# A decoder kernel on one core: first chunk in rounds, an output projection part, index queries and top-k rounds moved

## The chip, the cores and the metric

The kernel runs on one core of a Trainium2 chip, as one program. The metric is the device time of one execution in microseconds (us), lower is better. Five engines work from queues of their own and meet through semaphores: PE (TensorE matmuls; its weight loads are listed apart as PEld), DVE (VectorE), ACT (ScalarE), POOL (GpSimd) and SP (SyncE, which issues most DMAs). Each engine executes its own queue in order.

## What is computed

Two decoder layers over 512 tokens of width 1024 in float32, each a token mixer, a cross-attention into 256 memory tokens and a SwiGLU FFN, with a layer norm behind each. The mixer of layer 0 is latent attention (16 heads, low-rank queries and keys with RMS norms); that of layer 1 is sparse attention, where an indexer chooses 128 keys for each query:

```python
def mla_mixer(x, pos, w_in, q_norm, w_uq, kv_norm, w_ukv, w_o):
    h = x @ w_in                                  # c_q 512, c_kv 256, k_rope 32
    q = (rms_norm(c_q, q_norm) @ w_uq).reshape(b, s, 16, 64 + 32)
    kv = (rms_norm(c_kv, kv_norm) @ w_ukv).reshape(b, s, 16, 64 + 64)
    ...
    out = dense_causal_attention(q, k, v, (64 + 32) ** -0.5)
    return out.reshape(b, s, 16 * 64) @ w_o

def dsa_mixer(x, pos, rel_bias, w_in, w_o):
    h = x @ w_in                                  # q, k, v, 8 index queries, index key, weights
    ...
        dots = einsum('bqhd,bkd->bqhk', qi_blk, k_idx) * (64 ** -0.5)
        score = einsum('bqh,bqhk->bqk', wi_blk, relu(dots))
        score = where(causal, score, -inf)
        _, sel = lax.top_k(score, 128)
        ...
        logits = where(sel_ok, q_blk . k_sel * 64 ** -0.5 + rel_bias[bucket], -inf)
        o = softmax(logits) . v_sel
    return out @ w_o
```

## The kernel before

Every float32 product is made of three passes of a reduced type. `split` (ACT rounds to the high part, L104; a subtraction gives the low part, L106, on DVE or POOL) prepares an operand, and `mm3` (L137, L138, L139) adds high x high, high x low (or low x high) and the third. A weight chunk takes this path from DRAM: `raw` (a DMA), `wh` (ACT), `wl` (DVE or POOL). `bank("a")` and `bank("b")` are PSUM tiles (named `ps`), `t2` and `t8` SBUF tiles, `sm` small columns.

The code is handed to a scheduler at compile time, which sets the order of each engine's queue from a cost model and the data's dependences; `behind(ins)` pins an instruction after another in that order. The stages that the change touches, with their times in the profile:

- Start (0 to 20 us). `WARM` identity products on PE while the first DMAs land, then the first chunk: 4 token tiles times 8 chunks k of the width, 128x304 products into four banks (`ps2`).
- Latent norms (20 to 60 us). `rms_t` squares on ACT, takes the root on POOL, scales on DVE (L615) and transposes on PE (L618); `mla_v(i)` are value products. `rms_scaled`, the last scaled tile (`scaled[0]`), pins the split of a weight chunk that comes next (`wl_126`).
- Output projection of layer 0 (about 180 to 240 us). `out_proj_parts` is a generator that yields once, behind the products of its first weight chunk (c == 0); its caller continues it after the last heads' value products (L762, L763).
- Indexer (about 770 to 800 us). For each of four pairs j of index heads: a query projection (24 products), a split of the queries (`stack_q`), and scores for the query tiles qt = 1, 2, 3 (L1130, L1131); ACT takes the Relu (L1133), DVE adds them up into the tile's score (L1137).
- Top-k and sparse attention (about 800 to 935 us). The 128 largest of a row are taken away in 16 rounds of eight for each of qt = 1, 2, 3 (widths 256, 384, 512): `nc.vector.max` (L1149, MAX8 in the profile) and `match_replace` (L1150), on DVE, each reading what the one before left. `todo` holds the 48 rounds in order; 4 go before the key projections, `NTK[j]` before each query projection j = 0 to 7, the rest (`NTI` = 2 at a time) in the loop over n. `make_mask(qt)` (ACT, L1156) turns a finished tile into a mask.

Attention works on 16 items s0 to s15, item 4 qt + g for query tile qt and key head g, each of four query heads. Four names carry an item: `s` (scores: for each of the four heads a mask product L1205 where qt > 0, then L1206 and L1207 into a bank of ring "b", which has four; DVE reduces each bank, L498: scale, bias, row minimum; ACT takes the exponential, L505), `t` (transposes L1220 on PE into ring "a", split by L104 and L106), `p` (value products L1251, L1252; then L1254 on ACT, L1259 and L1263 on DVE). The score bank of one item comes free when DVE has reduced it, and the next item's products go there. `dsa_bias` loads the item's bias by a DMA from SP (L1186) into a `t8` tile. `steps` and `seq` order the items: s0 ... t2 s4, p2 t4 s5 behind the last query projections (j = 7), then s3, s6, s7, s8 and so on.

Of the kernel before, what the change touches and what calls it, by code (L numbers as in the profile page):

```python
# [15 lines left out]
ALU = mybir.AluOpType  # L16
# [7 lines left out]
NT = S // P  # L24
# [11 lines left out]
BIG = 2.0 ** 100  # L36
TOPK = 128
GW = 640
WARM = 8
NV = 256 + 8 + 64  # L40
NC0 = 256 + 32 + 16

# [27 lines left out]
def tile_hybrid_mla_dsa_deepnorm_block(ctx: ExitStack, tc: tile.TileContext, A: dict, out: bass.AP):  # L70
# [26 lines left out]
    def behind(ins):  # L97
        return tc.issue_after(ins.ins) if ins else ExitStack()

    high, low, load, power, scaled = ([None] for _ in range(5))  # L100

    def split(h, l, src, eng=None, after=None, copy_after=None):
        with behind(copy_after):
# [199 lines left out]
    def k_of(tiles, k):  # L303
        h, l = tiles[k // 4]
        return h[:, k % 4], l[:, k % 4]
# [87 lines left out]
    def out_proj_parts(src, w, kc, first, pins=(), pool=0):  # L393

        nk = 2 * kc

        def weights(n, c):
            pin = pins[kc * n + c] if pins else (None, None)
            return chunk(w(n, c), (P, 2, 512), nc.gpsimd if pin[1] or kc * n + c < pool else None, pin)

        for n in range(2):
            ws = [weights(n, c) for c in range(kc)] if n else None
            if n == 0:
                ps = [bank("b") for _ in range(NT)]
                for c in range(kc):
                    wh, wl = weights(n, c)
                    for i in range(2):
                        k = 2 * c + i
                        sh, sl = src(k)
                        for tt in range(NT):  # L410
                            ts_ = slice(P * tt, P * tt + P)
                            mm3(ps[tt], (sh[:, ts_], sl[:, ts_]), (wh[:, i], wl[:, i]), k == 0, k == nk - 1)
                    if c == 0:
                        norm = yield
                for tt in range(NT):
                    residual(ps[tt], tt, n, first)
                    if norm:
                        norm.stat(tt, n)
            else:
                for tt in range(NT):  # L420
                    ts_ = slice(P * tt, P * tt + P)
                    parts = TAIL if norm.last and tt == NT - 1 else ((0, 512),)
                    for c0, c1 in parts:
                        p1 = bank("b")
                        for k in range(nk):
                            sh, sl = src(k)
                            wh, wl = ws[k // 2]
                            mm3(p1[:, c0:c1], (sh[:, ts_], sl[:, ts_]), (wh[:, k % 2, c0:c1], wl[:, k % 2, c0:c1]), k == 0, k == nk - 1)
                        early = len(parts) > 1
                        if tt and c0 == 0 and not early:  # L430
                            norm.finish(tt - 1)
                        residual(p1, tt, n, first, c0, c1)
                        norm.stat(tt, n, c0, c1)
                        if c0 == 0 and early:
                            norm.finish(tt - 1)
                norm.finish(NT - 1)
# [53 lines left out]
    class Softmax:  # L490
# [4 lines left out]
        def exp(self, i, src, scale, in1=None, after=None):  # L495
            Sx, nb = self.parts[i], self.nb[:, i:i + 1]
            if in1 is not None:
                nc.vector.tensor_tensor_reduce(out=Sx, in0=src, in1=in1, op0=ALU.add, op1=ALU.min,  # L498
                                               scale=-scale, scalar=3e38, accum_out=nb)
                src, scale = Sx, -1.0  # L500
            else:
                nc.vector.tensor_reduce(nb, src, axis=AX.X, op=ALU.max)
                nc.vector.tensor_scalar(nb, nb, -scale, None, op0=ALU.mult)
            with behind(after):
                nc.scalar.activation(Sx, src, AF.Exp, bias=nb, scale=scale, accum_out=self.sm[:, i:i + 1])  # L505
# [15 lines left out]
    def ts_of(tt):  # L521
        return slice(P * tt, P * tt + P)
# [46 lines left out]
    for c in range(4):  # L569
        h, l = XT[c // 2]  # L570
        rx = raw_x[c // 2]
        step = 1 if c == 0 else 2
        for i in range(0, 2, step):
            k0 = 2 * (c % 2) + i
            split(h[:, k0:k0 + step], l[:, k0:k0 + step], rx[:, k0:k0 + step])
            if 2 * c + i in w_parts:
                t, a, b = w_parts[2 * c + i]
                split(whs[t][:, a:b], wls[t][:, a:b], raw_w[t][:, a:b])
        for i in range(2):
            k = 2 * c + i  # L580
            xh, xl = k_of(XT, k)
            for tt in range(NT):
                ts_ = ts_of(tt)
                mm3(ps2[tt][:, 0:NC0], (xh[:, ts_], xl[:, ts_]), (whs[k // 3][:, k % 3], wls[k // 3][:, k % 3]),
                    k == 0, k == NK - 1)
    steps = trig()
    next(steps)
    krs = []
# [55 lines left out]
    for tt in range(NT):  # L644
# [14 lines left out]
        if tt == 2:  # L659
            ka = t2()  # L660
            kb_ = t2()
            nc.vector.tensor_tensor(ka[0:64], pk[0:64], TK[0:64], op=ALU.mult)
            nc.vector.tensor_tensor(kb_[0:64], pk[64:128], TK[64:128], op=ALU.mult)
            nc.vector.tensor_tensor(ka[0:64], ka[0:64], kb_[0:64], op=ALU.add)
    for hv in range(5):
        mla_v(hv)
    rms_t(psq[NT - 1], 512, NT - 1, gq, cq)
    rms_end = high[0], low[0]
    rms_power, rms_scaled = power[0], scaled[0]

    K8 = [t8(), t8()]
    for i, k8 in enumerate(K8):
# [442 lines left out]
    KIA, KIB = t2(FR), t2(FR)  # L1115
    split(KIA, KIB, pk)
    masks = [None] + [t2() for _ in range(1, NT)]
    for j in range(4):
        pq = bank("a")
        proj(pq, chunk(A["w_qi"][j], (P, NK, P)), XT, (P, S))  # L1120
        qi = (t2(FR), t2(FR))
        stack_q(pq[:, P:], qi[0][:, P:], qi[1][:, P:])
        for qt in range(1, NT):
            n = P * (qt + 1)
            ts_ = slice(P * qt, P * qt + P)
# [13 lines left out]
            if j == 3:  # L1139
                nc.gpsimd.affine_select(out=acc[:, n - P:n], in_=acc[:, n - P:n], pattern=[[-1, P]],  # L1140
                                        compare_op=ALU.is_ge, fill=-1e30, base=0, channel_multiplier=1)
    MK = t8()

    def topk(qt, its):
        n = P * (qt + 1)
        acc = masks[qt]
        for it in its:
            m8 = tp.tile([P, 8], F32, tag="m8", name=nm("m8"), bufs=4)
            nc.vector.max(out=m8, in_=acc[:, :n])  # L1149
            nc.vector.match_replace(out=acc[:, :n], in_to_replace=m8, in_values=acc[:, :n], imm_value=-3e38)  # L1150

    def make_mask(qt, after=None):
# [4 lines left out]
        masks[qt] = mk  # L1157

    todo = [(qt, [i]) for qt in range(1, NT) for i in range(TOPK // 8)]
    NTK, NTI = (5, 5, 5, 5, 5, 4, 4, 4), 2  # L1160
    KA, KB = [], []
    for j in range(2):
        for _ in range(2):
# [130 lines left out]
    for j in range(8):  # L1294
# [12 lines left out]
        Q += [qa, qb]  # L1307
        for word in steps.get(j, "").split():
            run(word)

    for n in range(3, 16):
        if n + 2 < 16:
            run_s(seq[n + 2])
        if n + 1 < 16:
            run_t(seq[n + 1])
        dsa_pv(*items[seq[n]], *PT.pop(seq[n]))
        for _ in range(NTI):
            if todo:
                topk(*todo.pop(0))
        if n in (4, 8):  # L1320
            make_mask(2 + n // 8, outs[-1])

    pins = [(reads[max(4, 2 * c)] if c > 2 else None, spreads[1 + 2 * c] if c < 5 else None) for c in range(NK)]
    load_x(xsp)
# [90 lines left out]
```

## Time and profile before

| | us |
|---|---|
| median of 3 runs (1501.17 to 1501.28) | 1501.27 |
| profiled execution, its own time | 1501.13 |
| its span | 1499.3 |
| PE busy | 1475.3 (98%) |
| DVE busy | 1041.7 (69%) |
| ACT busy | 672.8 (45%) |
| POOL busy | 401.6 (27%) |

The page gives busy time by engine over the whole span, the share of each 40th of it, the chain of work that ended last and the costliest groups of instructions by line. A trace row has its start (us from the start of the span), its duration, engine, line, operation and, in brackets, the engine's idle time just before it and what ended it. L498 appears as two instructions of DVE (CUSTOM_DVE_ANT and a read of the accumulator). The tables of waits name the waiting tile and line and then what released it.

### The profile page before, as it was taken

Reading aid. Unit: us, or ns where it says so; the run is one execution under the profiler, and the core shown is the slowest. Engines: PE = TensorE matmul, PEld = TensorE weight load, DVE = VectorE, ACT = ScalarE, POOL = GpSimd, SP = SyncE. Lnnn points to the kernel's source line nnn. Section 1 sums busy time; section 2 is a strip of 40 time slices with the busy share of each in tenths; the row PEclk is TensorE's granted clock in tenths of the full one; section 3 lists DMA queues with packets and bytes.
Section 4 is the critical chain, followed back from the end, with each engine's and each line's share of the span. In section 5 each row is a group of like instructions: output and inputs, shape, how many; then the busy total and the mean of one; then the engine's idle time right before and its main releaser. Section 6 shows DMA issues by size and latency. Waiting matters only on the chain. (4 is left out here: it accounts for less than half of the span.)

```text
span 1499.3 us, 20324 instructions
## 1 busy us (share of the span) xinstructions
PE 1475.3 (98%) x7600; PEld 1258.1 (84%) x7600; DVE 1041.7 (69%) x1792; ACT 672.8 (45%) x1198; POOL 401.6 (27%) x368
## 2 busy tenths in 40 slices
PE   9999999999999999999999989999999999999998
PEld 8788888988888888888898768898889888888886
DVE  7766769667847656565778989685687575566656
ACT  4777743455233333333256688244542333334321
POOL 1454403010125223240025652030102233152302
PEclk9999999999999999999999999999999999999999
DMA  6244424423233332233333246353242333223231
GB/s 221 71 106 108 168 85 142 139 71 127 74 105 100 120 99 97 96 99 114 105 127 94 68 149 225 113 169 99 71 141 71 99 101 124 97 91 121 71 98 57
DMA packets 50282, 166.17 MB, mean 111 GB/s; under 512 B 5189, under 2 KB 11605, under 8 KB 47365
## 3 DMA queue, kind: packets, MB, share of 16 engines
q1 hardware_dynamic: 49460, 163.35, 33.6%
q10 hardware_dynamic: 720, 1.51, 0.3%
q8 instruction: 60, 0.98, 0.3%
q14 instruction: 42, 0.34, 0.1%
HBM read 160.60 MB, written 9.47 MB: 113 GB/s over the span
## 5 line engine op out<-in xcount | busy, mean ns | idle before, releaser
L137 PE MATMUL ps<-t,wh 128*128 128x512 f32 (+2 forms) x1184 | 433.3, 366 | 0.4 <-DVE t L106 0.3
L139 PE MATMUL ps<-t,wl 128*128 128x512 f32 (+2 forms) x1184 | 432.0, 365 | 1.4 <-DVE wl L106 1.4
L138 PE MATMUL ps<-t,wh 128*128 128x512 f32 (+2 forms) x1184 | 432.1, 365 | 0.0
L104 ACT CAST wh<-raw 128x1024 fp32r<-128x1024 f32 (+1 forms) x199 | 207.7, 1044 | 312.2 <-PE ps L138 136.5
L106 DVE TENSOR_TENSOR wl<-raw,wh 128x1024 fp32r<-128x1024 f32 (+2 forms) x170 | 234.8, 1384 | 108.9 <-ACT wh L104 108.0
L137 PE MATMUL ps<-wh,t 128*128 128x512 f32 (+2 forms) x736 | 281.7, 383 | 0.0
L138 PE MATMUL ps<-wl,t 128*128 128x512 f32 (+2 forms) x736 | 279.9, 380 | 0.1
L139 PE MATMUL ps<-wh,t 128*128 128x512 f32 (+2 forms) x736 | 279.5, 380 | 0.0
L139 PEld LDWEIGHTS ps<-t,wl 128*128 128x128 f32 x1184 | 223.3, 189 | 36.8 <-DVE wl L106 1.7
L137 PEld LDWEIGHTS ps<-t,wh 128*128 128x128 f32 x1184 | 223.3, 189 | 36.6 <-DVE t L106 1.6
L138 PEld LDWEIGHTS ps<-t,wh 128*128 128x128 f32 x1184 | 223.4, 189 | 34.5
L104 ACT CAST t<-ps 128x512 fp32r<-128x512 f32 (+3 forms) x241 | 118.2, 524 | 134.9 <-PE ps L368 85.9
L104 ACT CAST wh<-t 128x1024 fp32r<-128x1024 f32 (+1 forms) x84 | 82.3, 980 | 199.4 <-PE ps L138 163.8
L106 DVE TENSOR_TENSOR t<-ps,t 128x512 fp32r<-128x512 f32 (+3 forms) x241 | 137.8, 604 | 32.6 <-ACT t L104 31.4
L139 PEld LDWEIGHTS ps<-wh,t 128*128 128x128 f32 x736 | 138.5, 188 | 25.5
L137 PEld LDWEIGHTS ps<-wh,t 128*128 128x128 f32 x736 | 138.7, 188 | 24.9 <-ACT t L104 0.2
L138 PEld LDWEIGHTS ps<-wl,t 128*128 128x128 f32 x736 | 138.6, 188 | 24.9 <-DVE wl L106 0.5
L106 DVE TENSOR_TENSOR wl<-t,wh 128x1024 fp32r<-128x1024 f32 (+1 forms) x84 | 101.4, 1208 | 77.8 <-ACT wh L104 76.3
L300 POOL TENSOR_TENSOR sm<-sm,mhalf 128x1 f32<-128x1 f32 x32 | 28.3, 883 | 435.9 <-DVE sm L298 435.9
L104 ACT CAST t<-t 128x512 fp32r<-128x512 f32 (+3 forms) x133 | 75.4, 573 | 84.1 <-POOL t L944 51.6
L1015 DVE TENSOR_TENSOR t<-ps,t 128x512 f32<-128x512 f32 x44 | 30.4, 692 | 115.4 <-PE ps L139 115.4
L106 DVE TENSOR_TENSOR t<-t,t 128x512 fp32r<-128x512 f32 (+3 forms) x112 | 86.1, 775 | 33.1 <-ACT t L104 30.4
(184 smaller groups left out, 1924.8 us busy)
## 6 DMA issues: line engine op xcount, KB each, us to landing
raw<-in_ffn_in_dram SPq DMA_DIRECT2D x88, 512.0 KB, 3.5
t<-in_ffn_dg_dram SPq DMA_DIRECT2D x16, 1024.0 KB, 5.1
raw<-in_xa_k_dram SPq DMA_DIRECT2D x16, 512.0 KB, 3.6
raw<-in_xa_v_dram SPq DMA_DIRECT2D x16, 512.0 KB, 4.1
raw<-in_xa_q_dram SPq DMA_DIRECT2D x16, 512.0 KB, 3.6
scr<-vscr SPq DMA_DIRECT2D x16, 319.5 KB, 4.2
raw<-in_w_uq_dram SPq DMA_DIRECT2D x8, 512.0 KB, 3.9
raw<-in_mla_o_dram SPq DMA_DIRECT2D x8, 512.0 KB, 5.5
```

Source lines behind the costliest of these rows:

```text
L104: high[0] = nc.scalar.copy(h, src)
L106: low[0] = (eng or nc.vector).tensor_tensor(l, src, h.bitcast(F32), op=ALU.subtract)
L137: nc.tensor.matmul(ps, st[0], mv[0], start=start, stop=False, skip_group_check=more)
L138: nc.tensor.matmul(ps, st[0], mv[1], start=False, stop=False, skip_group_check=more)
L139: return nc.tensor.matmul(ps, st[1], mv[0], start=False, stop=stop, skip_group_check=more)
L300: power[0] = nc.gpsimd.tensor_tensor(b, a, mhalf, op=ALU.pow)
L1015: nc.vector.tensor_tensor(sg, pu, sg, op=ALU.mult)
```

## The change

Five edits. (1) `WARM` 8 becomes 9, and the first chunk's (k == 0) products run in three rounds over the four token tiles: all high x high, then high x low, then low x high. (2) `out_proj_parts` yields behind its second weight chunk (c == 1). (3) `rms_scaled` is taken before the value products and the last `rms_t`, so it names an earlier scaled tile. (4) The index queries of pair j + 1 are written ahead of the scores of pair j (`index_queries`, `index_scores`). (5) `reduced[0]` holds the last L498 reduction; `NTK` ends in 2 instead of 4, two rounds stand behind the j loop pinned to `reduced[0]`, which then is the last reduction of s5, and `make_mask` is called at n = 3 and 7 instead of 4 and 8.

In what follows, lines of the changed kernel are up to 18 higher (L1149 is L1165, L1150 L1166, L1205 L1221, L1220 L1236, L1259 L1275, L1263 L1279); `t2_1503` is the score tile of qt = 3, `m8` holds a round's eight values, and the numbers in `ps` names count up with the items.

DVE, before, between the reductions of s4 (the first row is its last accumulator, width 256) and the first reductions of s5 (`t8_1758`):

```order
L498 ISA sm_1725_11499 128x1
L1149 MAX m8_1784_11711<-t2_1503_10574 128x8
L1150 MATCH_REPLACE t2_1503_10574<-m8_1784_11711,t2_1503_10574 128x512
L1149 MAX m8_1801_11774<-t2_1503_10574 128x8
L1150 MATCH_REPLACE t2_1503_10574<-m8_1801_11774,t2_1503_10574 128x512
L1149 MAX m8_1802_11777<-t2_1503_10574 128x8
L509 RECIPROCAL sm_1751_11593<-sm_1726_11500 128x4
L1150 MATCH_REPLACE t2_1503_10574<-m8_1802_11777,t2_1503_10574 128x512
L1149 MAX m8_1823_11848<-t2_1503_10574 128x8
L1150 MATCH_REPLACE t2_1503_10574<-m8_1823_11848,t2_1503_10574 128x512
L1149 MAX m8_1824_11851<-t2_1503_10574 128x8
L1259 TENSOR_TENSOR t2_1748_11585<-ps_1746_11580,t2_1747_11583 64x256 x2
```

DVE, changed, from the same row of s4 to the last reduction of s5 (`t8_1756` here):

```order
L498 ISA sm_1725_11500 128x1
L509 RECIPROCAL sm_1749_11588<-sm_1726_11501 128x4
L498 ISA t8_1756_11613,sm_1757_11615<-ps_1759_11617,t8_1756_11613 128x256
L498 ISA sm_1757_11615 128x1
L1275 TENSOR_TENSOR t2_1746_11580<-ps_1744_11575,t2_1745_11578 64x256 x2
L498 ISA t8_1756_11613,sm_1757_11615<-ps_1760_11623,t8_1756_11613 128x256
L498 ISA sm_1757_11615 128x1
L1279 TENSOR_TENSOR t2_1746_11580<-t2_1746_11580,ps_1747_11583 128x256
L498 ISA t8_1756_11613,sm_1757_11615<-ps_1761_11629,t8_1756_11613 128x256
L498 ISA sm_1757_11615 128x1
L498 ISA t8_1756_11613,sm_1757_11615<-ps_1762_11635,t8_1756_11613 128x256
L498 ISA sm_1757_11615 128x1
```

The rounds that stood between the two items are gone from there; `reduced` pins the next round behind s5, and since each round reads what the last one left, all later rounds follow it.

DVE, before, ahead of the reductions of s8 (`t8_1825`, width 384):

```order
L509 RECIPROCAL sm_1811_11810<-sm_1787_11717 128x4
L1150 MATCH_REPLACE t2_1503_10574<-m8_1824_11851,t2_1503_10574 128x512
L1259 TENSOR_TENSOR t2_1799_11763<-ps_1797_11756,t2_1798_11761 64x256 x2
L1149 MAX m8_1844_11922<-t2_1503_10574 128x8
L1263 TENSOR_TENSOR t2_1799_11763<-t2_1799_11763,ps_1800_11766 128x256
L1150 MATCH_REPLACE t2_1503_10574<-m8_1844_11922,t2_1503_10574 128x512
L106 TENSOR_TENSOR t2_1814_11819<-ps_1812_11813,t2_1813_11818 128x512
L106 TENSOR_TENSOR t2_1817_11828<-ps_1815_11822,t2_1816_11827 128x512
L1259 TENSOR_TENSOR t2_1821_11837<-ps_1819_11832,t2_1820_11835 64x256 x2
L1263 TENSOR_TENSOR t2_1821_11837<-t2_1821_11837,ps_1822_11840 128x256
L498 ISA t8_1825_11854,sm_1826_11856<-ps_1828_11858,t8_1825_11854 128x384
```

DVE, changed, ahead of the same reductions:

```order
L509 RECIPROCAL sm_1811_11811<-sm_1787_11719 128x4
L1165 MAX m8_1823_11849<-t2_1503_10575 128x8
L1166 MATCH_REPLACE t2_1503_10575<-m8_1823_11849,t2_1503_10575 128x512
L106 TENSOR_TENSOR t2_1814_11820<-ps_1812_11814,t2_1813_11819 128x512
L106 TENSOR_TENSOR t2_1817_11829<-ps_1815_11823,t2_1816_11828 128x512
L1275 TENSOR_TENSOR t2_1821_11838<-ps_1819_11833,t2_1820_11836 64x256 x2
L1165 MAX m8_1824_11852<-t2_1503_10575 128x8
L1279 TENSOR_TENSOR t2_1821_11838<-t2_1821_11838,ps_1822_11841 128x256
L1166 MATCH_REPLACE t2_1503_10575<-m8_1824_11852,t2_1503_10575 128x512
L1165 MAX m8_1844_11923<-t2_1503_10575 128x8
L1166 MATCH_REPLACE t2_1503_10575<-m8_1844_11923,t2_1503_10575 128x512
L498 ISA t8_1825_11855,sm_1826_11857<-ps_1828_11859,t8_1825_11855 128x384
```

Of the rounds of qt = 3, one and a half stood between the last reduction of s5 and the first of s8 (`MATCH_REPLACE` of m8_1824, then the round m8_1844); now nine stand there (m8_1763, 1764, 1783, 1784, 1801, 1802, 1823, 1824, 1844), three of their instructions right ahead of s8.

PE, before, at the end of the scores of s11 (`ps_1895`), with transposes of s9 (`ps_1879`, `ps_1882`) and value products of s9 (`ps_1885`):

```order
L1205 MATMUL ps_1895_12104<-t8_1576_10876,identb_85 128x384
L1206 MATMUL ps_1895_12104<-t8_1590_10960,t2_1740_11569 128x384
L1220 MATMUL ps_1879_12043<-ident_69,t8_1845_11925 128x128 x4
L1207 MATMUL ps_1895_12104<-t8_1590_10960,t2_1740_11569 128x384
L1220 MATMUL ps_1882_12052<-ident_69,t8_1845_11925 128x128 x4
L1251 MATMUL ps_1885_12061<-t2_1855_11962,t8_1485_10411 128x512
L1252 MATMUL ps_1885_12061<-t2_1856_11963,t8_1485_10411 128x512
```

PE, changed, the same place; `ps_1914` is the first bank of s12:

```order
L1221 MATMUL ps_1895_12105<-t8_1576_10877,identb_86 128x384
L1222 MATMUL ps_1895_12105<-t8_1590_10961,t2_1738_11564 128x384
L1236 MATMUL ps_1879_12045<-ident_69,t8_1845_11926 128x128 x4
L1223 MATMUL ps_1895_12105<-t8_1590_10961,t2_1738_11564 128x384
L1221 MATMUL ps_1914_12166<-t8_1576_10877,identb_86 128x512
L1222 MATMUL ps_1914_12166<-t8_1583_10915,t8_1591_10970 128x512
L1223 MATMUL ps_1914_12166<-t8_1583_10915,t8_1591_10970 128x512
L1236 MATMUL ps_1882_12054<-ident_69,t8_1845_11926 128x128 x4
L1221 MATMUL ps_1915_12172<-t8_1576_10877,identb_86 128x512
```

The first three score products of s12 moved ahead of the last transposes of s9.

The diff:

```diff
--- before.py
+++ after.py
@@ -36,7 +36,7 @@
 BIG = 2.0 ** 100
 TOPK = 128
 GW = 640
-WARM = 8
+WARM = 9
 NV = 256 + 8 + 64
 NC0 = 256 + 32 + 16
 
@@ -97,7 +97,7 @@
     def behind(ins):
         return tc.issue_after(ins.ins) if ins else ExitStack()
 
-    high, low, load, power, scaled = ([None] for _ in range(5))
+    high, low, load, power, scaled, reduced = ([None] for _ in range(6))
 
     def split(h, l, src, eng=None, after=None, copy_after=None):
         with behind(copy_after):
@@ -410,7 +410,7 @@
                         for tt in range(NT):
                             ts_ = slice(P * tt, P * tt + P)
                             mm3(ps[tt], (sh[:, ts_], sl[:, ts_]), (wh[:, i], wl[:, i]), k == 0, k == nk - 1)
-                    if c == 0:
+                    if c == 1:
                         norm = yield
                 for tt in range(NT):
                     residual(ps[tt], tt, n, first)
@@ -495,8 +495,8 @@
         def exp(self, i, src, scale, in1=None, after=None):
             Sx, nb = self.parts[i], self.nb[:, i:i + 1]
             if in1 is not None:
-                nc.vector.tensor_tensor_reduce(out=Sx, in0=src, in1=in1, op0=ALU.add, op1=ALU.min,
-                                               scale=-scale, scalar=3e38, accum_out=nb)
+                reduced[0] = nc.vector.tensor_tensor_reduce(out=Sx, in0=src, in1=in1, op0=ALU.add, op1=ALU.min,
+                                                            scale=-scale, scalar=3e38, accum_out=nb)
                 src, scale = Sx, -1.0
             else:
                 nc.vector.tensor_reduce(nb, src, axis=AX.X, op=ALU.max)
@@ -579,10 +579,15 @@
         for i in range(2):
             k = 2 * c + i
             xh, xl = k_of(XT, k)
+            wh, wl = whs[k // 3][:, k % 3], wls[k // 3][:, k % 3]
+            if k == 0:
+                for n, (x_, w_) in enumerate(((xh, wh), (xh, wl), (xl, wh))):
+                    for tt in range(NT):
+                        nc.tensor.matmul(ps2[tt][:, 0:NC0], x_[:, ts_of(tt)], w_, start=n == 0, stop=False)
+                continue
             for tt in range(NT):
                 ts_ = ts_of(tt)
-                mm3(ps2[tt][:, 0:NC0], (xh[:, ts_], xl[:, ts_]), (whs[k // 3][:, k % 3], wls[k // 3][:, k % 3]),
-                    k == 0, k == NK - 1)
+                mm3(ps2[tt][:, 0:NC0], (xh[:, ts_], xl[:, ts_]), (wh, wl), False, k == NK - 1)
     steps = trig()
     next(steps)
     krs = []
@@ -662,11 +667,12 @@
             nc.vector.tensor_tensor(ka[0:64], pk[0:64], TK[0:64], op=ALU.mult)
             nc.vector.tensor_tensor(kb_[0:64], pk[64:128], TK[64:128], op=ALU.mult)
             nc.vector.tensor_tensor(ka[0:64], ka[0:64], kb_[0:64], op=ALU.add)
+    rms_scaled = scaled[0]
     for hv in range(5):
         mla_v(hv)
     rms_t(psq[NT - 1], 512, NT - 1, gq, cq)
     rms_end = high[0], low[0]
-    rms_power, rms_scaled = power[0], scaled[0]
+    rms_power = power[0]
 
     K8 = [t8(), t8()]
     for i, k8 in enumerate(K8):
@@ -1115,11 +1121,14 @@
     KIA, KIB = t2(FR), t2(FR)
     split(KIA, KIB, pk)
     masks = [None] + [t2() for _ in range(1, NT)]
-    for j in range(4):
+    def index_queries(j):
         pq = bank("a")
         proj(pq, chunk(A["w_qi"][j], (P, NK, P)), XT, (P, S))
         qi = (t2(FR), t2(FR))
         stack_q(pq[:, P:], qi[0][:, P:], qi[1][:, P:])
+        return qi
+
+    def index_scores(j, qi):
         for qt in range(1, NT):
             n = P * (qt + 1)
             ts_ = slice(P * qt, P * qt + P)
@@ -1139,14 +1148,21 @@
             if j == 3:
                 nc.gpsimd.affine_select(out=acc[:, n - P:n], in_=acc[:, n - P:n], pattern=[[-1, P]],
                                         compare_op=ALU.is_ge, fill=-1e30, base=0, channel_multiplier=1)
+
+    waiting = index_queries(0)
+    for j in range(4):
+        ahead_q = index_queries(j + 1) if j < 3 else None
+        index_scores(j, waiting)
+        waiting = ahead_q
     MK = t8()
 
-    def topk(qt, its):
+    def topk(qt, its, after=None):
         n = P * (qt + 1)
         acc = masks[qt]
         for it in its:
             m8 = tp.tile([P, 8], F32, tag="m8", name=nm("m8"), bufs=4)
-            nc.vector.max(out=m8, in_=acc[:, :n])
+            with behind(after):
+                nc.vector.max(out=m8, in_=acc[:, :n])
             nc.vector.match_replace(out=acc[:, :n], in_to_replace=m8, in_values=acc[:, :n], imm_value=-3e38)
 
     def make_mask(qt, after=None):
@@ -1157,7 +1173,7 @@
         masks[qt] = mk
 
     todo = [(qt, [i]) for qt in range(1, NT) for i in range(TOPK // 8)]
-    NTK, NTI = (5, 5, 5, 5, 5, 4, 4, 4), 2
+    NTK, NTI = (5, 5, 5, 5, 5, 4, 4, 2), 2
     KA, KB = [], []
     for j in range(2):
         for _ in range(2):
@@ -1307,6 +1323,8 @@
         Q += [qa, qb]
         for word in steps.get(j, "").split():
             run(word)
+    for _ in range(2):
+        topk(*todo.pop(0), reduced[0])
 
     for n in range(3, 16):
         if n + 2 < 16:
@@ -1317,8 +1335,8 @@
         for _ in range(NTI):
             if todo:
                 topk(*todo.pop(0))
-        if n in (4, 8):
-            make_mask(2 + n // 8, outs[-1])
+        if n in (3, 7):
+            make_mask(2 + n // 7, outs[-1])
 
     pins = [(reads[max(4, 2 * c)] if c > 2 else None, spreads[1 + 2 * c] if c < 5 else None) for c in range(NK)]
     load_x(xsp)
```

## The prediction, made before the changed kernel ran

> **What bounds the kernel now.** I read the head of the page first, then PE's waits, then stretches of the trace around the largest of them.
>
> ```profile
> span 1499.3 us, 20324 instructions
> PE 1475.3 (98%) x7600; PEld 1258.1 (84%) x7600; DVE 1041.7 (69%) x1792; ACT 672.8 (45%) x1198; POOL 401.6 (27%) x368
> ```
>
> PE works 98% of the span: 24.0 us (1499.3 - 1475.3) is all that it does not. The change removes no product and adds one identity product, so nothing can be gained but part of those 24 us and what a low clock costs. PE's waits (total us, times, longest):
>
> ```profile
> PE ps L1206 <- DVE sm L498: 2.6, 1, 2.6
> PE ps L139 <- DVE wl L106: 1.4, 1, 1.4
> PE ps L762 <- DVE t L106: 1.1, 1, 1.1
> PE ps L1205 <- ACT t L1156: 0.7, 2, 0.5
> ```
>
> The first and the last lie in the sparse attention. Busy time by stretch there, with the granted clock (PEclk):
>
> ```profile
> core 0: us, PE busy (x) PEld busy (x) DVE busy (x) ACT busy (x) POOL busy (x), PEclk, DMA share, GB/s
> 799.00:851.00 52.00, 50.34 (x232) 40.71 (x232) 49.65 (x149) 34.32 (x65) 31.44 (x22) 1.00 0.27 87
> 851.00:861.50 10.50, 10.50 (x57) 8.97 (x56) 10.18 (x32) 7.03 (x19) 6.08 (x12) 1.00 0.17 52
> 865.00:870.00 5.00, 2.72 (x13) 2.51 (x14) 4.66 (x20) 2.77 (x9) 4.69 (x7) 0.78 0.19 79
> 870.00:875.00 5.00, 5.00 (x35) 4.69 (x35) 3.39 (x17) 4.55 (x17) 0.40 (x1) 0.88 0.18 41
> 875.00:885.00 10.00, 8.10 (x46) 6.12 (x46) 8.81 (x27) 7.97 (x21) 5.80 (x11) 1.00 0.40 137
> 885.00:890.00 5.00, 3.67 (x23) 3.19 (x22) 4.45 (x19) 4.45 (x13) 4.28 (x7) 1.00 0.87 308
> 890.00:905.00 15.00, 13.43 (x80) 11.11 (x80) 12.41 (x36) 13.27 (x34) 6.97 (x16) 1.00 0.48 168
> 905.00:930.00 25.00, 24.94 (x143) 20.52 (x142) 23.59 (x63) 21.60 (x51) 6.01 (x18) 1.00 0.81 281
> ```
>
> From 799 to 861.5 both engines are full: PE works through the query projections, DVE through the top-k rounds (49.65 of 52, 10.18 of 10.5). From 865 PE has no projections left and works to DVE's pace. Where one turns into the other, s5 waits:
>
> ```profile
> 862.85 0.36 PE L1205 MATMUL ps<-t,identb 128*128 128x256 f32 x1
> ...
> 863.67 0.69 DVE L1149 MAX8 m<-t 128x8 f32<-128x512 f32 x1
> ...
> 864.23 0.28 PE L1207 MATMUL ps<-t,t 128*128 128x256 f32 x1
> ...
> 865.19 0.69 DVE L1149 MAX8 m<-t 128x8 f32<-128x512 f32 x1
> ...
> 866.66 0.42 DVE L498 CUSTOM_DVE_ANT_0 t<-ps,t 128x256 f32<-128x256 f32 x1
> ...
> 867.15 0.39 PE L1206 MATMUL ps<-t,t 128*128 128x256 f32 x1 [2.64 <-DVE sm L498]
> ```
>
> PE finished s5's scores about 864.5; DVE had rounds ahead of the reduction and began it at 866.66; the next product needed that bank. A 512-wide round takes 1.52 us (865.19 - 863.67).
>
> **Edit 5, the rounds.** Undoing this wait is the gain on offer: 2.6 us, plus the clock. PEclk 0.78 and 0.88 is a loss of at most 5 x (0.22 + 0.12) = 1.7 us, and starts right behind the wait. On that, "TensorE: Matmul & The Clock Gate" of the Trainium skill, section "Why this matters for your kernels", asks for no idle gap of more than about 3 us; here 2.64 us went with the drop, so the row is harsher than the rule. By the rule the new gap of about 4 us found below would cost the clock too, and the old one would not have.
>
> The price is where the rounds go. The reductions of s5 have to wait for s5's scores, and those come only when PE is through the projections: 862.85, less 0.7 (edit 4, below), less 0.85 for s0, whose reductions also come one 384-wide round sooner:
>
> ```profile
> 834.95 1.50 PE L1220 MATMUL ps<-ident,t 128*128 128x128 f32 x4
> ```
>
> Four transposes take 0.63 us unhindered (the row at 892.03 below), so about 0.85 us of the 1.50 was waiting for s0's exponentials. So s5's scores start near 861.3 and its first bank is full, three 256-wide products (0.12 us each) on, at 861.7. The order puts nine rounds behind s5 that used to be one and a half, and each reads the one before, so DVE has about 7 us with nothing to do in 851 to 861.5, where it was full. It pays them back between s5 and s8. What it did there before (busy, mean ns, idle before):
>
> ```profile
> L498 DVE CUSTOM_DVE_ANT_0 t<-ps,t 128x256 f32<-128x256 f32 x12 | 4.8, 417 | 1.7 <-PE ps L1207 1.6
> L106 DVE TENSOR_TENSOR t<-ps,t 128x512 fp32r<-128x512 f32 x6 | 4.1, 689 | 0.8 <-ACT t L104 0.7
> L1259 DVE TENSOR_TENSOR t<-ps,t 64x256 f32<-64x256 f32 x8 | 3.3, 414 | 0.2 <-ACT t L1254 0.2
> L1263 DVE TENSOR_TENSOR t<-t,ps 128x256 f32<-128x256 f32 x4 | 1.7, 414 | 0.1
> L1149 DVE MAX8 m<-t 128x8 f32<-128x512 f32 x2 | 1.4, 695 | 0.1
> L1150 DVE MATCH_REPLACE8 t<-m,t 128x512 f32<-128x512 f32 x2 | 1.4, 676 | 0.0
> L498 DVE CUSTOM_DVE_ANT_0 t<-ps,t 128x128 f32<-128x128 f32 x4 | 1.1, 285 | 0.3 <-PE ps L1207 0.3
> ```
>
> ```profile
> 884.93 0.55 DVE L498 CUSTOM_DVE_ANT_0 t<-ps,t 128x384 f32<-128x384 f32 x1
> ```
>
> From 866.66 to 884.93 are 18.27 us, of which 3.2 idle (the last column) and 2.2 one and a half rounds: 12.9 us of other work. Now the two L1259 of p4 stand inside the stretch (0.85), and nine rounds cost 9 x 1.52 = 13.7: 27.4 us. Its inputs are there: PE was busy 15.8 us (2.72 + 5.00 + 8.10) from 865 to 885, through the same items and partly at the low clock. So s8's reductions start at 861.7 + 27.4 = 889.1, against 884.93: **4.2 us later**. PE, which needs s8's first bank for s9, stands idle for about 4 us before it. The gain of the 2.6-us wait is in this number already: PE gets to wait later and longer. Bounds: 3.5 if pitches overlap more, 5.0 if they overlap less.
>
> Behind s8 the same order runs as before, and a lag can be made up only out of PE's idle time from 885 to 905, 2.9 us (5 - 3.67, and 15 - 13.43). What sets it:
>
> ```profile
> 892.03 0.63 PE L1220 MATMUL ps<-ident,t 128*128 128x128 f32 x4
> ...
> 892.80 7.22 SPq L1186 DMA_DIRECT2D t<-scr  x2
> ...
> 897.39 0.56 DVE L498 CUSTOM_DVE_ANT_0 t<-ps,t 128x384 f32<-128x384 f32 x1 [0.72 <-PE ps L1220]
> ...
> 898.87 0.30 PE L1220 MATMUL ps<-ident,t 128*128 128x128 f32 x1 [1.33 <-DVE t L1259]
> ```
>
> s11's bias takes the tile that s8's last transposes (892.03) read: issued 892.80, its reduction runs at 897.39, and PE waits until 898.87. That chain hangs on s8 and shifts whole. Recovered are the three 512-wide products of s12 that now run inside this wait (3 x 0.23 = 0.7) and up to 0.4 of the mask waits (the L1205 row), since masks 2 and 3 are asked for one step earlier: together 1.1, at least 0, at most the 2.9. From 905 to 930 PE is busy 24.94 of 25: nothing comes back there.
>
> The idle gap before s9 (about 4 us) is longer than the one that went with the low clock. What the old drop cost is inside 884.93 already; a new one behind 890 adds 0 (where PE waits for DVE anyway) to 1.7: I take the middle, 0.9.
>
> **Edit 4, index queries.** At 775.75 and three places like it PE passes from a query projection to the scores:
>
> ```profile
> 775.75 0.34 PE L138 MATMUL ps<-t,wh 128*128 128x384 f32 x1
> ...
> 776.11 0.39 PE L1130 MATMUL ps<-t,t 128*128 128x256 f32 x1
> ```
>
> 0.36 us from start to start where neighbours take 0.17: 0.19 us, four times 0.7 us. With the next pair's projection between, the split is long done. DVE's rounds start as much sooner. Counted above in 861.3; bounds 0 and 0.8.
>
> **Edit 3, `rms_scaled`.**
>
> ```profile
> 46.92 4.74 POOL L106 TENSOR_TENSOR wl<-raw,wh 128x1024 fp32r<-128x1024 f32 x2
> ...
> 50.09 2.66 DVE L106 TENSOR_TENSOR wl<-raw,wh 128x1024 fp32r<-128x1024 f32 x1
> ...
> 52.80 0.50 PE L139 MATMUL ps<-t,wl 128*128 128x512 f32 x1 [1.38 <-DVE wl L106]
> ```
>
> DVE's split of `wl_126` runs beside POOL's of the same shape and takes 2.66 us, ending 1.1 after POOL's. "SBUF — State Buffer" of the Trainium skill ("Terms") calls the port pair of the two engines a lock held for a whole instruction; this trace agrees. The split now stands six rows earlier in DVE's order, ahead of the last L615, so the 1.4-us wait goes. But that L615 tile then comes behind it, and on ACT the high part of another chunk ahead of the tile's cast, so the query products that read it are late next: I take -0.3, between -1.4 (the whole wait) and +1.3 (a split of 2.66 us, less 1.4, in the path of the norms).
>
> **Edits 1 and 2.** The first chunk no longer needs its low weights for the second product, worth some 0.5 us, but
>
> ```profile
> 10.43 0.41 PE L139 MATMUL ps<-wh,t 128*128 128x304 f32 x1
> ```
>
> is k = 2's third product, started 0.15 after its neighbour where 0.14 is the pace: it runs as its low half of x arrives, which no edit moves, so what is saved ahead is waited here: 0, between -0.5 and +0.4 (one more identity product ahead of an operand that is already there). The later yield puts 24 products (24 x 0.23 = 5.4 us) ahead of the last heads' value products; the one wait at L762 (1.1) is for an operand of the pair before; covered by the products themselves: 0, and +1.1 if what follows the value products is late.
>
> **The sum.** +4.2 (s8) - 1.1 (recovered) + 0.9 (clock) - 0.3 (edit 3) = +3.7 us on the profiled 1501.13, which lies 0.14 under the median: 1504.8. What a measurement can tell from no change is 0.2%, 3.0 us.
>
> **Rivals.** *The lag is absorbed (faster).* If DVE makes good the 4.2 us before PE is full at 905, by the 2.9 us of PE's idle time and the 1.7 of the clock, and edits 1 to 3 bring 1.5, the time is 1501.1 + 4.2 - 2.9 - 1.7 - 1.5 = 1499.2. Under 1498.1, where it counts as faster, it comes only if the stretch up to s8 takes 26.3 instead of 27.4 us, that is, from rounds of 1.40 instead of 1.52 us down; at 1.2 us it is 1496.3. For it: DVE idles 3.2 us between s5 and s8 and 2.6 from 890 to 905. Against: the rounds are one chain on the engine that the reductions need. *The rounds make no difference.* s8 lags by 4.2 and all PE idle time up to 905 takes it up, within 2 us of before: 1501 to 1503. *Clock twice.* PE is idle for about half of 865 to 890, in gaps; each drop like the old one costs up to 1.7 us, and a full and a second one behind s9 would give 1504.8 + 0.8 + 1.7 = 1507.3. The page on the clock gate (Trainium skill) lets an idle window, not the average, decide, by which one drop remains.
>
> **Chances.** Slower as summed 0.38, with the clock twice 0.09; lag largely taken up 0.33; faster 0.20. Slower by over 0.2% is so 0.47, within it 0.33, faster 0.20. The range goes from 1497.0, half of the faster rival, to 1508.0, which holds the clock twice but for a few hundredths; the likeliest case's own is 1503.5 to 1506.5.
>
> **What would show it.** Right: DVE without work before s5; its reductions at 861.5 to 862, no 2.6-us L1206 wait, no low clock at 868; s8's reductions at 888.5 to 890; PE waiting 3 to 4 us at an L1221 for a reduction L498; PE full from about 908. Wrong: s8 before 887, or a lag at 905 of under 1 us. Edit 4 is wrong if the 0.19-us gaps remain, edit 3 if a wait of over 1 us stands at 50 to 61.

## The result, and the profile after

The changed kernel takes 1509.65 us (median of 6 runs, 1508.73 to 1511.48) against 1501.28 (6 runs, 1500.69 to 1501.64): 8.4 us slower, ratio 1.0057, 95% interval [1.0044, 1.007]. The profiled execution has a span of 1508.5 us, 9.2 more than before; it took 1510.43 us, 0.8 above the median, so sums over the traces come out that much above 8.4.

The head of its page:

```profile
span 1508.5 us, 20329 instructions
PE 1480.6 (98%) x7602; PEld 1259.5 (83%) x7602; DVE 1041.2 (69%) x1792; ACT 672.8 (45%) x1198; POOL 404.1 (27%) x368
```

PE is busy 5.3 us longer with two more records in its row (one more identity product): a product that runs at the low clock counts as busy for longer (0.63 instead of 0.40 us for one of 512 columns at L139 in the rows at 50 us). PE's waits (total, times, longest):

```profile
PE ps L1221 <- DVE sm L498: 3.1, 6, 1.1
PE ps L137 <- ACT t L104: 3.0, 1, 3.0
...
PE ps L1139 <- ACT t L1142: 0.8, 3, 0.4
```

The 2.6-us wait of L1206 is gone, and so is the 1.4-us wait of L139 for `wl`. New are a wait of 3.0 us of a projection for ACT and several of L1221 for a reduction. Setting each product of PE beside the product of the same place before gives where the time went: the lag is under 0.2 us from 20 to 48 us, 4.5 at 100, 4.6 at 760, 4.8 at 800, 4.9 at 855, 9.8 at 889, and 9.2 from 975 to the end. Two places made it: 45 to 60 us, and 862 to 890 us.

**At 50 us.** ACT, changed; the three rows are the last latent-value cast, the cast of a query weight chunk (`wh_210`), and the cast of the last latent-query tile:

```profile
50.83 0.37 ACT L104 CAST t<-ps 128x256 fp32r<-128x256 f32 x1 [0.34 <-PE ps L139]
53.80 1.04 ACT L104 CAST wh<-raw 128x1024 fp32r<-128x1024 f32 x1 [2.59 <-DMA raw<-in_w_uq_dram]
54.75 0.58 ACT L104 CAST t<-ps 128x512 fp32r<-128x512 f32 x1
```

PE has transposed that tile by 51.7 (the row below), but its cast stands behind a cast that waits for a DMA. The DMA had been issued late, once POOL had freed a `raw` buffer (its first split, shown further down, ends at about 50.3):

```profile
51.11 0.60 PE L623 MATMUL ps<-ident,t 128*128 128x128 f32 x4
```

```profile
50.32 0.80 SPq L118 DMA_DIRECT2D raw<-in_w_uq_dram  x2
```

PE then stood still, and ran the products behind the wait at half the clock (three 512-wide ones take 1.65 us; at the full clock, in the run with the cast pinned below, three take 0.97):

```profile
52.00 0.40 PE L139 MATMUL ps<-t,wl 128*128 128x512 f32 x1
55.38 1.65 PE L137 MATMUL ps<-t,wh 128*128 128x512 f32 x3 [2.98 <-ACT t L104]
...
57.68 0.63 PE L139 MATMUL ps<-t,wl 128*128 128x512 f32 x1
```

```profile
55.00:60.00 5.00, 4.62 (x11) 3.67 (x12) 3.93 (x5) 2.62 (x5) 4.33 (x3) 0.50 0.45 163
60.00:65.00 5.00, 5.00 (x24) 4.19 (x23) 2.67 (x4) 1.48 (x2) 0.55 (x1) 0.88 0.01 3
```

Before, the clock was 1.00 in both stretches:

```profile
55.00:60.00 5.00, 4.90 (x23) 3.92 (x21) 3.60 (x5) 2.24 (x4) 4.67 (x3) 1.00 0.24 90
60.00:65.00 5.00, 4.59 (x23) 3.96 (x24) 4.31 (x10) 3.63 (x8) 2.41 (x1) 1.00 0.52 159
```

**At 860 to 895 us.** Busy time by stretch, changed (columns as before: PE, PEld, DVE, ACT, POOL, PEclk). From 851 to 861.5 DVE works 8.14 us, where it was full before:

```profile
851.00:861.50 10.50, 9.28 (x51) 7.51 (x49) 8.14 (x28) 6.78 (x18) 8.26 (x10) 1.00 0.01 2
...
905.00:930.00 25.00, 23.89 (x131) 18.93 (x131) 22.38 (x63) 21.40 (x53) 9.33 (x21) 1.00 0.77 270
```

The first reduction of s5 and that of s8 on DVE, and the first product of s9 on PE:

```profile
868.38 0.42 DVE L498 CUSTOM_DVE_ANT_0 t<-ps,t 128x256 f32<-128x256 f32 x1 [2.83 <-PE ps L1223]
...
894.70 0.55 DVE L498 CUSTOM_DVE_ANT_0 t<-ps,t 128x384 f32<-128x384 f32 x1
...
895.31 0.45 PE L1221 MATMUL ps<-t,identb 128*128 128x384 f32 x1 [1.14 <-DVE sm L498]
```

Less the lag of 4.9 that came with them, s5 is reduced at 863.5 (866.66 before) and s8 at 889.8 (884.93 before): 4.9 us later, as the nine rounds behind s5 let one expect.

A low clock lies ahead of s9, behind a wait of 1.26 us, and is over when s9's products start at 895.31:

```profile
890.26 1.71 PE L1236 MATMUL ps<-ident,t 128*128 128x128 f32 x8 [1.26 <-DVE t L106]
```

```profile
890.00:892.50 2.50, 2.24 (x10) 1.87 (x11) 2.46 (x6) 0.49 (x1) 0.00 (x0) 0.63 0.00 1
892.50:895.00 2.50, 1.68 (x5) 0.88 (x4) 2.43 (x7) 0.00 (x0) 1.37 (x4) 0.68 0.61 176
895.00:897.50 2.50, 2.19 (x12) 2.05 (x12) 2.50 (x12) 2.21 (x7) 0.59 (x2) 1.00 1.05 418
```

PE waited another 1.14 us for s8's reduction behind it, so this low clock did not delay s9.

### The profile page after: what moved, and what is told of

It reads as the page before. It is cut to its first block, busy times and chain, and to the rows that moved or that the text cites. A ratio compares the mean times of both kernels' runs of the same rounds, so it can differ in the third digit from the quotient of the medians.

```text
span 1508.5 us, 20329 instructions
## 1 busy us (share of the span) xinstructions
PE 1480.6 (98%) x7602; PEld 1259.5 (83%) x7602; DVE 1041.2 (69%) x1792; ACT 672.8 (45%) x1198; POOL 404.1 (27%) x368
## 4 chain that ended last, share of the span: by engine, by line
PE 86%; DVE 6%; ACT 3%; issue 2%; DMA 2%; POOL 1%; DVEq 0%; SPq 0%; ACTq 0%; POOLq 0%
PE ps L137 27%; PE ps L138 27%; PE ps L139 26%; DVE t L1166 1%; PE ps L368 1%; DVE m L1165 1%; PE ps L741 1%; ACT t L505 1%; DVE t L106 1%; ACT t L104 1%; DMA raw<-in_w_cq_dram 1%; PE ps L768 1%; ACT wh L104 1%; PE ps L769 1%; PE ps L1236 1%
## 5 line engine op out<-in xcount | busy, mean ns | idle before, releaser
L139 PE MATMUL ps<-t,wl 128*128 128x512 f32 (+2 forms) x1184 | 432.6, 365 | 0.0
L106 DVE TENSOR_TENSOR wl<-raw,wh 128x1024 fp32r<-128x1024 f32 (+2 forms) x170 | 233.5, 1376 | 110.4 <-ACT wh L104 109.7
L137 PE MATMUL ps<-wh,t 128*128 128x512 f32 (+3 forms) x732 | 280.1, 383 | 0.0
L138 PE MATMUL ps<-wl,t 128*128 128x512 f32 (+3 forms) x732 | 278.5, 380 | 0.0
L139 PE MATMUL ps<-wh,t 128*128 128x512 f32 (+3 forms) x732 | 277.9, 380 | 0.6 <-DVE t L106 0.6
L139 PEld LDWEIGHTS ps<-t,wl 128*128 128x128 f32 x1184 | 223.8, 189 | 35.3
L106 DVE TENSOR_TENSOR t<-ps,t 128x512 fp32r<-128x512 f32 (+3 forms) x241 | 138.2, 605 | 35.6 <-ACT t L104 34.7
L139 PEld LDWEIGHTS ps<-wh,t 128*128 128x128 f32 x732 | 137.5, 188 | 26.4 <-DVE t L106 0.8
L106 DVE TENSOR_TENSOR wl<-t,wh 128x1024 fp32r<-128x1024 f32 (+1 forms) x84 | 101.5, 1208 | 78.6 <-ACT wh L104 77.0
L104 ACT CAST t<-t 128x512 fp32r<-128x512 f32 (+3 forms) x133 | 75.6, 574 | 85.1 <-POOL t L950 51.7
L106 DVE TENSOR_TENSOR t<-t,t 128x512 fp32r<-128x512 f32 (+3 forms) x112 | 86.0, 774 | 33.2 <-ACT t L104 30.4
```

Of the source, the lines that this page charges most:

```text
L104: high[0] = nc.scalar.copy(h, src)
L106: low[0] = (eng or nc.vector).tensor_tensor(l, src, h.bitcast(F32), op=ALU.subtract)
L137: nc.tensor.matmul(ps, st[0], mv[0], start=start, stop=False, skip_group_check=more)
L138: nc.tensor.matmul(ps, st[0], mv[1], start=False, stop=False, skip_group_check=more)
L139: return nc.tensor.matmul(ps, st[1], mv[0], start=False, stop=stop, skip_group_check=more)
```

## Experiments

Times are medians; a difference in us is the ratio to the kernel before, run on the same chip, times its time (1501.2, 1500.8 and 1501.3 us in the three sets).

**Edit 3 alone.**

```diff
+    rms_scaled = scaled[0]
     for hv in range(5):
         mla_v(hv)
     rms_t(psq[NT - 1], 512, NT - 1, gq, cq)
     rms_end = high[0], low[0]
-    rms_power, rms_scaled = power[0], scaled[0]
+    rms_power = power[0]
```

> Edit 3 alone. Theory A (queue order on ACT): the cast of the next query weight chunk stands ahead of the cast of the last latent-query tile and waits there for its own DMA, so the query products start 3 us late and the clock drops behind that wait; the lag stays to the end: +4.4 us on the kernel before (1505.6), a wait of 2.5 to 3.5 us at an L137 near 52, PEclk near 0.5 for 55 to 60. Rival (the whole cost belongs to edit 5 and the trace's lag at 57 comes back later): within 1.5 us of before.

1504.85 us, ratio 1.0022 [1.0013, 1.0031]: +3.3 us. PE's wait and the clock:

```profile
PE ps L137 <- ACT t L104: 3.0, 1, 3.0
```

```profile
55.00:60.00 5.00, 4.76 (x14) 3.77 (x15) 4.08 (x5) 2.48 (x5) 4.33 (x3) 0.66 0.41 150
```

The cost is edit 3's own: 3.0 of wait less the 1.4 that went, and 5 x 0.34 = 1.7 us of clock, make 3.3. The size is a little below the 4.4 expected, which had taken the changed kernel's clock of 0.50.

**Edit 3 with the cast pinned.** One pin more: the high cast of the third query weight chunk goes behind that of the last latent-query tile.

```diff
-    def chunk(src, shape, eng=None, after=(None, None)):
+    def chunk(src, shape, eng=None, after=(None, None), cast_after=None):
...
-        split(h[:, :n], l[:, :n], raw[:, :n], eng, after[1])
+        split(h[:, :n], l[:, :n], raw[:, :n], eng, after[1], cast_after)
...
-            wts["q"] = chunk(A["w_uq"][pr], (P, 4, 256), nc.gpsimd, (None, rms_power if pr < 2 else None))
+            wts["q"] = chunk(A["w_uq"][pr], (P, 4, 256), nc.gpsimd, (None, rms_power if pr < 2 else None),
+                             rms_end[0] if pr == 2 else None)
```

> Edit 3 alone, with one thing more: the high cast of the third query weight chunk is pinned behind the high cast of the last latent-query tile on ACT. Theory A: the 3-us wait and the low clock are gone, and the early split of wl_126 takes the old 1.4-us wait away: 0 to -1.4 us on before (1499.9 to 1501.3). Rival B (the early split itself costs, by holding POOL's root and its two splits back 1 us, so that the weight DMAs land 1 us later): +2 to +4 us, with a wait at the same place on a DMA or on a weight's low part.

1499.73 us, ratio 0.9989 [0.998, 0.9998]: -1.7 us, a little more than the 0 to -1.4 expected. ACT takes the tile at once, DVE's early split takes 1.22 instead of 2.66 us, and PE's longest wait behind it is 0.6 (one of 0.7 for L615 ahead of it stands in both kernels):

```profile
51.72 0.59 ACT L104 CAST t<-ps 128x512 fp32r<-128x512 f32 x1 [0.53 <-PE ps L618]
```

```profile
52.36 0.97 PE L137 MATMUL ps<-t,wh 128*128 128x512 f32 x3
```

```profile
46.29 1.22 DVE L106 TENSOR_TENSOR wl<-raw,wh 128x1024 fp32r<-128x1024 f32 x1
```

```profile
PE ps L139 <- DVE t L106: 0.6, 1, 0.6
```

This tells the theories apart: the early split is a gain, POOL's delay costs nothing here, and the loss comes from one instruction's place in ACT's queue. (The pin without edit 3 was not run.) In the profiled execution PE is 1.0 to 1.2 us ahead of before from 57 to 866 us; another 1 us comes at 868 to 870, where the clock stayed at 1.00 in this execution (last section), so not all of the 1.7 need be the edit's own. Rival B did see something real. In the changed kernel POOL's root of 0.55 us takes 1.48 beside DVE's split, and its weight splits start at 47.90 instead of 46.92, so the DMA that waits for their buffer is issued at 50.32 instead of 49.35. Where ACT's cast waits for that DMA, about 1 of the 2.59 us is this delay (an estimate from these four starts):

```profile
46.44 1.48 POOL L300 TENSOR_TENSOR sm<-sm,mhalf 128x1 f32<-128x1 f32 x1 [1.03 <-DVE sm L298]
47.90 4.75 POOL L106 TENSOR_TENSOR wl<-raw,wh 128x1024 fp32r<-128x1024 f32 x2
```

"SBUF — State Buffer" of the Trainium skill ("Terms") has the shared port pair held for a full instruction, with the loser blocked; the 1.48 us agree, POOL's op ending 0.4 us behind DVE's (46.29 + 1.23), less than its own 0.55.

**Edit 5 alone.** `reduced`, `NTK` ending in 2, two pinned rounds, masks at n = 3 and 7, as in the diff of the change.

> Edit 5 alone. Theory C (nine rounds in a chain behind s5 hold DVE, s8's reductions come 4 to 5 us later, PE has no idle time behind 905 to make it up): +3.5 to +5 us on before (1504.8 to 1506.3). Rival D (the lag of the changed kernel at 895 comes from edits 4 and 5 together, since rounds start at another time): +1 to +2.5 us.

1506.9 us, ratio 1.0032 [1.0021, 1.0043]: +4.8 us, which is theory C. DVE, PE and the clock:

```profile
863.51 0.42 DVE L498 CUSTOM_DVE_ANT_0 t<-ps,t 128x256 f32<-128x256 f32 x1 [2.84 <-PE ps L1208]
...
889.83 0.55 DVE L498 CUSTOM_DVE_ANT_0 t<-ps,t 128x384 f32<-128x384 f32 x1
```

```profile
890.44 0.44 PE L1206 MATMUL ps<-t,identb 128*128 128x384 f32 x1 [2.15 <-DVE sm L498]
```

```profile
887.50:890.00 2.50, 0.78 (x5) 0.26 (x3) 2.43 (x7) 0.00 (x0) 1.37 (x4) 1.00 0.82 247
890.00:892.50 2.50, 2.06 (x9) 2.06 (x10) 2.50 (x12) 2.08 (x7) 0.46 (x2) 0.81 1.05 423
892.50:895.00 2.50, 1.84 (x7) 1.36 (x7) 1.95 (x7) 2.48 (x7) 2.50 (x2) 0.50 0.16 64
895.00:897.50 2.50, 2.50 (x12) 2.40 (x11) 2.33 (x8) 2.45 (x8) 0.11 (x1) 0.50 0.00 0
```

From s5 to s8 are 26.3 us (forecast: 27.4), as in the changed kernel, and s8 is late by 4.9. The gap ahead of s9 is only 2.15 us, but PE worked 0.78 of the 2.5 us around it, and the clock was low from 891.6 to about 898. "TensorE: Matmul & The Clock Gate" of the Trainium skill ("Why this matters for your kernels") sets the limit at gaps of about 3 us; this row does not agree, as the 2.64 us before did not.

**Edits 1, 2 and 4 together**, without 3 and 5.

> Edits 1, 2 and 4, without 3 and 5. If the lag of the changed kernel is 4.4 us from edit 3 and 4.5 from edit 5, these three give -0.7 to +0.5 us on before. As forecast, edit 4 alone would give -0.7; by the trace of the changed kernel its four gaps came back as waits for the Relu's banks: 0 to +0.3.

1501.61 us, ratio 0.9999 [0.999, 1.0008]: no difference for the three together (none was run alone). The four gaps between projection and scores are gone, and in their place the scores wait for their banks, which ACT's Relu (L1141 here) empties:

```profile
PE ps L1138 <- ACT t L1141: 0.8, 3, 0.4
```

**Edit 5 with the last rounds left out.** `todo` is cut to its first 41 of 48 rounds; the last query tile's mask then keeps 72 keys instead of 128.

```diff
-    todo = [(qt, [i]) for qt in range(1, NT) for i in range(TOPK // 8)]
+    todo = [(qt, [i]) for qt in range(1, NT) for i in range(TOPK // 8)][:41]
```

> Edit 5 alone, with the last 7 of the 16 rounds of the last query tile left out (its mask keeps 72 keys), so that two of the nine rounds remain behind s5. Theory C (the chain of rounds on DVE sets s8): s8's reductions come 7 x 1.52 = 10.6 us earlier than in edit 5 alone, then PE bounds; -3.5 to -6 us on before (1495 to 1498). Rival D (not the rounds but the new order of the items, or the clock, costs): at least 1503.

1499.64 us, ratio 0.9989 [0.998, 0.9998]: -1.7 us, a miss in size. The rounds are the cause of edit 5's loss, since without seven of them it is gone. (The 1.7 us are no gain to be had: the kernel before does all 48 rounds.) But s8's reductions come 6.8 us sooner than in edit 5 alone, not 10.6:

```profile
883.08 0.55 DVE L498 CUSTOM_DVE_ANT_0 t<-ps,t 128x384 f32<-128x384 f32 x1
```

```profile
863.80:883.08 19.28, 16.78 (x99) 12.66 (x98) 16.58 (x60) 15.97 (x46) 12.34 (x20) 1.00 0.37 128
```

From s5 to s8 DVE is busy 16.58 us, 8.7 less than with nine rounds (25.30), and stands idle for 2.7 of 19.28 us, 1.69 of them in one wait for ACT (L1255). So the stretch has a second bound just below DVE's, the way of each item through the other engines; which step of it sets the pace was not taken apart. Seven rounds are worth 6.5 us of the kernel's time.

**Three rounds behind s5** (`NTK` ending in 8, the two pinned rounds, masks as before).

```diff
-    NTK, NTI = (5, 5, 5, 5, 5, 4, 4, 4), 2
+    NTK, NTI = (5, 5, 5, 5, 5, 4, 4, 8), 2
...
+    for _ in range(2):
+        topk(*todo.pop(0), reduced[0])
```

> Edit 5 without its mask part and with 8 as the last number of NTK: three of the nine rounds stand behind s5 instead of all nine, and three fill DVE's idle time between s4 and s5. Theory C: s5 is reduced as soon as in edit 5, s8 is late by only 1.5 more rounds than before (2.3 us) against 3.1 us that s5 gains: -1 to -3 us on before (1498.3 to 1500.3), no wait of 2.6 us and no low clock at 868. Rival D: about as edit 5 alone, +3 or more.

1501.62 us, ratio 1.0005 [0.9996, 1.0014]: no difference, where 1 to 3 us of gain were expected. DVE is full ahead of s5 and reduces it at 864.12, 2.5 us sooner than before; the 2.6-us wait and the low clock are gone. What PE waits for from 862 to 882 instead, and its busy time there (clock 1.00; second fence: before, clock 0.91):

```profile
PE ps L1221 <- ACT t L111: 0.7, 1, 0.7
PE ps L1221 <- DVE t L106: 0.6, 1, 0.6
PE ps L1206 <- DVE sm L498: 0.5, 2, 0.3
PE ps L1206 <- ACT t L1157: 0.5, 1, 0.5
PE ps L1221 <- DVE t L1260: 0.5, 1, 0.5
PE ps L1253 <- DVE t L106: 0.3, 1, 0.3
PE ps L110 <- ACT t L109: 0.3, 1, 0.3
```

```profile
862.00:882.00 20.00, 16.56 (x98) 12.27 (x97) 17.36 (x63) 16.37 (x46) 11.97 (x19) 1.00 0.36 120
```

```profile
862.00:882.00 20.00, 16.35 (x102) 14.23 (x100) 17.61 (x63) 15.77 (x47) 12.59 (x20) 0.91 0.40 131
```

These are 3.4 us in all, and before PE waits 3.4 us there too: the one of 2.6, and 0.5 for the mask and 0.3 for L106, which stand in both. So one wait became six of 2.6 us together, and PE has done no more by 882 (98 records against 102). s8's reductions come at 885.20, 0.3 later than before: the stretch from s5 to s8 took 21.08 us instead of 18.27, with DVE (third figure of busy time) busy 17.64 instead of 15.20:

```profile
864.12:885.20 21.08, 17.45 (x98) 12.81 (x97) 17.64 (x63) 16.16 (x46) 12.16 (x20) 1.00 0.33 115
```

```profile
866.66:884.93 18.27, 15.75 (x90) 13.27 (x91) 15.20 (x56) 15.29 (x45) 9.29 (x17) 0.91 0.27 86
```

The one and a half rounds more in it took back most of the 2.5 us that s5 had gained. That the small waits had been hidden under the large one is a reading of the list; no run shows it apart from the rounds.

**Six rounds behind s5** (`NTK` ending in 5).

> The same with 5 as the last number: six rounds behind s5, none between s4 and s5. Theory C: three rounds more than with 8, 3 x 1.52 = 4.6 us later at s8, part of it below PE's own work: +1 to +3 us on before (1502.3 to 1504.3). Rival D: as edit 5 alone (+4.8).

1503.67 us, ratio 1.0018 [1.0009, 1.0027]: +2.7 us. With three, six and nine rounds behind s5 the kernel takes +0.8, +2.7 and +4.8 us: about 0.67 us for each round. From s5's first reduction to s8's, with six and with nine rounds (three are shown above):

```profile
863.90:887.42 23.52, 18.97 (x99) 14.41 (x98) 21.34 (x71) 16.28 (x46) 12.36 (x20) 0.93 0.31 106
```

```profile
863.51:889.83 26.32, 19.51 (x104) 13.18 (x102) 25.30 (x81) 16.30 (x46) 13.76 (x24) 1.00 0.35 115
```

A round takes DVE 1.28 us here ((25.30 - 17.64) / 6) and not 1.52. Back to back, each instruction of a round starts behind the end of the last (before: 863.67 + 0.69, then 864.40); here another item's instruction starts 0.61 us behind a MAX8 of 0.69 (edit 5 alone, 866.37). Of the 1.28, DVE's idle time (3.44, 2.18 and 1.02 us) gives 0.40 back, and the stretch grows by 0.87 a round.

**Early masks alone**, the part of edit 5 that the last two left out.

> Only the third part of edit 5: the masks of the last two tiles are asked for at n = 3 and 7 instead of 4 and 8. Forecast: up to -0.4 us (the waits of L1205 for L1156, 0.7 us in the profile before), so no difference that can be measured; if the early mask were the cost of edit 5, +2 us or more.

1500.78 us, ratio 0.9998 [0.9988, 1.0007]: no difference.

**The whole change with the cast pinned.**

> The whole change, with the pin of the third query weight chunk's cast on ACT added. If the queue order on ACT is the cost of edit 3 in the changed kernel too, and the parts add up: 4.9 us less than the changed kernel (edit 3 alone +3.3, with the pin -1.6), 1504.5 to 1505.5. If edit 5's low clock and edit 3 depend on each other: above 1507.

1504.71 us, ratio 1.0024 [1.0014, 1.0033]: +3.6 us, 4.9 us below the changed kernel's 1509.65. The same pin does the same in the full change; the parts add up (-1.7 + 4.8 - 0.2 = +2.9, within the intervals). That 1504.71 lies on the forecast of 1504.8 is in part luck, since several terms of the sum were off and made up for each other (next section).

**Edit 1, edit 3 with the pin, early masks.**

> The parts that did not cost anything, together: edit 1, edit 3 with the pinned cast, and the early masks. -1.6 (edit 3 with the pin) - 0.3 (masks) - 0.1 (edit 1): -1.5 to -2.5 us on before (1498.5 to 1499.7).

1499.29 us, ratio 0.9988 [0.9979, 0.9997]: -1.8 us. The best version that the parts point to, ahead of both kernels, though by no more than edit 3 with the pin alone.

## Why the prediction was right and wrong

- **Slower, and by the rounds on DVE:** right. s8's reductions were forecast 4.2 us late and were 4.9; edit 5 costs 4.8 us. What was behind it was a little off. The stretch took 26.3 us instead of 27.4: the nine rounds were priced at 1.52, back to back, and took 1.28 between other work (9 x 1.28 + 12.9 + 0.85 = 25.3, DVE's busy time), with 1.0 idle on top. And s5 came at 863.5 instead of 861.7, because neither edit 4's 0.7 nor s0's 0.85 arrived (s0's reductions came at 837.74, 4.94 us later than before on a lag of 4.8, so no round sooner). PE's idle gap of about 4 us ahead of s9 did not come either: the wait there was 1.14 us (2.15 in edit 5 alone), and the lateness was spread over several waits (six at L1221 for reductions, 3.1 us).
- **Edit 3:** this is the step that failed. "I take -0.3, between -1.4 and +1.3": it costs 3.3 alone, and the lag is 4.5 us in the changed kernel at 100 us. Its own sign of being wrong, a wait of over 1 us at 50 to 61, came true with 2.98. The prediction saw the right row of the order (the cast of another chunk ahead of the tile's cast on ACT) and named what is late next, but priced it as the length of a busy instruction. It waited 2.59 us for a DMA that had only just been issued, and the low clock behind the wait was left out. Without this term the time is inside the range: with the cast pinned the whole change takes 1504.71.
- **The clock:** +0.9 was taken behind s9. In edit 5 alone the clock fell there (0.77 in 890 to 905); in the changed kernel's trace it fell ahead of s9, where PE then waited for DVE all the same, and s9 was no later for it. The drop that cost time came at 55 us, where none was forecast. The rival "clock twice" had the number of drops right and both places wrong; PE was not idle for half of 865 to 890 but for 4.8 of 25 us.
- **Recovered behind s8:** 1.1 forecast; in the changed kernel the lag falls from 9.8 at 889 to 9.2 at 975, 0.6.
- **Edits 1, 2 and 4:** 0 was forecast for the first two, and the three together gave nothing that can be measured. Of edit 4 the four gaps went as said, but no time was gained: the products then waited for the Relu.
- **The lag is absorbed, or the rounds make no difference:** did not happen. PE had 1.1 us idle from 905 to 930 and 0.1 in the 30 us behind, and the lag stayed.

Open: a round behind s5 lengthens the stretch to s8 by 0.87 us and costs the kernel 0.67; where the rest goes, and which step of the items' way is the second bound, was not taken apart.

## What to carry to other kernels

A cast that moves up in an in-order queue is priced by when its operand arrives, not by its length: look up the DMA that feeds it, when its buffer comes free, and who stands behind it. A wait of 2.6 us on a bounding engine is worth what the next constraint leaves of it; here, with the rounds moved behind it, its removal was worth nothing that can be measured, and a run with the suspected work left out showed that a next bound was near. Work that fills an engine's idle time should stay in front of the point where that engine starts to set the pace.

## Unexpected of the hardware

PE's clock fell behind a wait of 2.15 us (edit 5 alone), 2.64 us (before) and 3.0 us (edit 3); in the first PE was busy 0.78 of the 2.5 us ahead, and the low clock lasted some 6.5 us (0.81, 0.50, 0.50 in three stretches of 2.5 us and 0.82 in the next). In the changed kernel it fell behind a wait of only 1.26 us (890.26). So with scattered idle time a shorter gap was enough.

The length of a wait does not decide it alone. The wait for s5's reduction, 2.63 to 2.71 us, stands in the kernel before and in five of the runs. The clock fell behind it in four of the six (0.78 before) and stayed at 1.00 in two, here edit 3 with the cast pinned:

```profile
866.02 0.39 PE L1208 MATMUL ps<-t,t 128*128 128x256 f32 x1 [2.66 <-DVE sm L498]
```

```profile
865.00:870.00 5.00, 3.84 (x26) 3.34 (x27) 4.71 (x23) 3.90 (x14) 3.60 (x5) 1.00 0.00 2
```

What else decides it was not tested. Each run has one profiled execution, so a drop in one trace is no property of the kernel, and in a sum the low clock belongs as a range.
